# Half of a causal convolution's taps as products with diagonal tiles

## The chip, the cores and the metric

The kernel runs on one core of a Trainium2 chip. The metric is device time in microseconds (us) of one execution, as the median of several runs. TensorE (PE in the profile) multiplies tiles and writes PSUM; VectorE (DVE), ScalarE (ACT) and GpSimd (POOL) work element by element; SyncE (SP) issues the transfers.

## What is computed

A block with three mixers side by side (causal depthwise convolution, pooling, differential attention) and a routed mixture of 16 experts is followed by two layers of another kind. 256 tokens pass through it. The change touches the convolution of the first block only:

```
u = a_val * sigmoid(a_gate)                      # [256 tokens, 256 channels]
y[t, ch] = b_dw[ch] + sum over j of w[j, ch] * u[t - 30 + j, ch]     # 31 taps, zeros before t = 0
y = silu(layer_norm(y)); y @ w_pw + b_pw
```

All of it is float32. `a_val` and `a_gate` are columns of the product of the normed input with `w_in`, as are the inputs of the pooling and the attention's q, k and v. The three mixers' outputs, side by side, are multiplied by `w_out` and added to the residual.

## The kernel before

Activations lie with features on the 128 partitions and tokens along the row. Each weight is cut into two parts, a rounded one (`h`, on ScalarE, line 361) and the rest (`l`, on VectorE or for some sections on GpSimd, line 377), and each product of a 128x128 weight tile is three matmuls (lines 485 to 487). Weights stream in, in order of use, and are split six chunks of four tiles ahead of the products, into 9 buffers for `h` and 7 for `l`.

The order of the first block's work is written as a weave. A generator (`fillers`) puts out the products, and after every four weight tiles (12 matmuls) there is a tick. At a tick, work that was put off with `after(n, ...)` comes due, `conv_tick` takes one step of each running convolution, and up to two attention events are taken (scores, turned probabilities, values). What comes out is an order of emission; a scheduler of the compiler turns it into one fixed order for each engine, and may move an instruction ahead when what it needs is there.

The products of `w_in` come in this order: the values (a section of its own, ticks 2 to 9), then 14 output tiles of two ticks each: q0, k0, a0, gate 0, a1, gate 1, q1, k1, q2, k2, q3, k3, p0, p1 (ticks 10 to 37). Each output tile is summed in one of the four PSUM buffers of the pool `mm`. The norm's factor for each token (line 605: `norm_rows`) is worked out by a chain of small VectorE instructions (lines 524 to 537) at the start of the 14 tiles. The convolution of channels 0 to 127 starts when gate 0 is done (tick 17), the other half at tick 21. Heads 0 and 1 of the attention get their q and k normed after k1, heads 2 and 3 after k3, each by a chain of small VectorE instructions (`norm_qk`) and products with them (line 598).

A step of a convolution is one tap on VectorE: `y = u * w + y` over 128x256 (line 983). Of the 31 taps, 18 go this way. The other 13 are multiplied on ScalarE (lines 972 and 977) and added up on GpSimd (line 978), one in each of the first steps; a last VectorE addition (line 985) joins the two sums. Two steps after both halves are done the layer norm follows (`conv_norm`). Then come the products with `w_pw` and `w_out`, which wait for the mixers' outputs, the last of them for the last two heads of the attention.

Of the kernel before, what the change touches and what calls it, by code (L numbers as in the profile page):

```python
# [36 lines left out]
TAPS = 18  # L37
# [3 lines left out]
# ---------------------------------------------------------------- tile order  # L41
def order(ms, kc, first):
    """Output tiles `ms` over kc input chunks: the first group chunk by chunk, the rest
    one output tile after the other."""
    out = [(k, m) for k in range(kc) for m in ms[:first]]
    for m in ms[first:]:
        out += [(k, m) for k in range(kc)]
    return out
# [17 lines left out]
def moe_order():  # L66
    """Weight pieces of the experts as they are used: ("in", e), and ("down", e) LAG experts later."""
    out = []
    for e in range(16 + LAG):
        out += [("in", e)] if e < 16 else []  # L70
        out += [("down", e - LAG)] if e >= LAG else []
    return out
# [5 lines left out]
def z_columns():  # L78
    """Columns of w_in_2 for each tile of Z_MS; in branches A and C chunk i holds heads i and i + 4.
    Rotary partners lie 32 features apart."""  # L80
# [16 lines left out]
def sections():  # L97
    """The weight stream, section by section: name, number of 128x128 tiles."""
# [16 lines left out]
# ---------------------------------------------------------------- host layout  # L115
def cut(w, plan, rows=None, cols=None):
    """Tiles [n, 128, 128] of w in the order of plan."""
# [58 lines left out]
def columns(v):  # L176
    """A vector over features as columns of 128 features."""
# [40 lines left out]
def lay_rpb(rpb):  # L218
    """[layers, pairs, query chunks, 128, 2 heads, T]: bias of every key, NEG where it isn't seen."""
# [12 lines left out]
def shared_tables():  # L232
    """Constants that depend on shapes alone, up to 128 rows each."""
# [85 lines left out]
# ---------------------------------------------------------------- the program  # L319
class Stream:  # L320
    """Weights in order of use: loaded ahead, cut in two parts a few chunks ahead of the products."""
# [12 lines left out]
    def widen(self, pool, bufs, until):  # L334
        """More buffers for the units before `until`."""
# [3 lines left out]
    def load(self, to=None):  # L339
        """Units up to `to`, or as many as there is room for."""  # L340
# [29 lines left out]
    def rest(self, c):  # L370
        """The second parts of the chunks before c that have their first."""
# [18 lines left out]
class Weave:  # L390
    """Puts other work between the pieces of a run of products. An event says whether it could take place."""
# [16 lines left out]
    def run(self, fill, events=(), first=0, last=1):  # L408
        """Ticks with each piece of fill; the events are spread over ticks first to last, counted from here."""
# [18 lines left out]
class Kernel:  # L428
# [36 lines left out]
    # -------- weights  # L465
# [5 lines left out]
    def weight4(self, t):  # L471
        """Four tiles in a row, as one moving operand."""
        return self.stream.chunk(t // CHUNK)

    def mm_w(self, out, xh, xl, wh, wl, start, stop):
        """The activations stay, the weights move."""
# [12 lines left out]
    def linear(self, name, plan, kc, xh, xl, n, evac, at=0, every=0, bank=None):  # L489
        """Yields after each output tile (or every so many products); evac(m, psum) takes the sum over the kc chunks.  # L490
        n: columns, or a function of m."""
# [18 lines left out]
    # -------- small helpers  # L510
# [8 lines left out]
    def rsqrt(self, src, shape, mul, add=EPS):  # L519
        """1 / sqrt(src * mul + add)."""  # L520
# [20 lines left out]
    def head_rsqrt(self, ssq, shape):  # L541
        """From sums over a head of squares without the token's 1 / rms: the factor that norms the head,
        1 / sqrt(ssq / HD + EPS / rms ** 2)."""
        return self.rsqrt(ssq, shape, 1.0 / HD, self.eps_tok.to_broadcast(shape))

    # -------- deferred rms norm
    def norm_chunk(self, k, n, gain, square=True):
        """Chunk k of the residual: x * gain in two parts, and its square added up."""
# [26 lines left out]
    def norm_tok(self, n, bank=None):  # L575
        """1 / rms of each token, tokens on the partitions: columns of tokens 0, 128 (and T - 128) on."""
# [12 lines left out]
    def spread(self, y, n):  # L589
        """Such columns on all partitions, tokens along the row (in psum). y: [128, 3], or [128, 3, 2] for a column for each  # L590
        half of the partitions."""
# [10 lines left out]
    def norm_rows(self, n, ticks=(2, 5)):  # L602
        """1 / rms of each token on all partitions: self.rb, within the next few ticks."""
# [18 lines left out]
    # -------- block 2  # L622
    def ffn(self, f, l, n, gain, n_next, ticks=(2, 5)):
        """X += 0.5 * swiglu, then what the next norm needs (the last one has its gain applied later)."""
# [60 lines left out]
class Block1:  # L685
    """Conv, pool and differential attention mixers side by side, then the routed experts."""
# [23 lines left out]
    def small(self):  # L710
# [5 lines left out]
        # lambda and scaled gains  # L716
# [42 lines left out]
    # -------- w_in, and the three mixers between its products and those of w_out  # L759
    def mixers(self):  # L760
# [14 lines left out]
        self.after(30, self.later_tables)  # L775
        self.after(6, self.lam)
# [56 lines left out]
    def out_tiles(self, name, ks):  # L833
        """Input chunks ks of the output tiles of w_out, two of which share a bank that the first one's start clears."""
# [35 lines left out]
    def turn_tokens(self, k):  # L870
        """Chunk k of x: its part of the router's products, and tokens on the partitions in two parts."""
# [53 lines left out]
    def norm_qk(self, first):  # L925
        """Norms of q and k of two heads."""
# [13 lines left out]
    def pool_mix(self, c, z):  # L940
        """Window means over 2, 4 (chunk 0) or 8, 16 (chunk 1) tokens less the token itself."""
# [23 lines left out]

    def conv_steps(self, c):
        """The taps of chunk c one by one: the last ones are summed apart, by other engines."""
        K, nc = self.K, self.nc
        tap = lambda j: (self.u[c][:, j:j + S], K.param("conv_w", 31 * c + j))
        y, other = self.cv[c], self.one([128, S], f"cw{c}")  # L970
        u, w = tap(TAPS)
# [931 lines left out]
```

## Time and profile before

| | |
|---|---|
| time, median of 3 runs | 1694.37 us (1693.71 to 1694.73) |
| span of the profiled execution (the only time that is shown of it) | 1698.4 us |
| TensorE busy | 1629.2 us, 96% of the span |
| VectorE busy | 1235.9 us, 73% |
| ScalarE busy | 990.8 us, 58% |
| GpSimd busy | 343.9 us, 20% |

Busy times are shares of the whole span; the stretch with the convolution is about its first twelfth. Times in the rows below are counted from the start of the span. "idle before <- releaser" is how long the engine had been idle before an instruction, and what ended that.

### The profile page before, as it was taken

How to read it: one execution, taken by the hardware profiler on the slowest of the kernel's cores; microseconds unless marked ns; L12 is line 12 of the kernel's file. 1: busy time of each engine (PE TensorE's matmuls, PEld its weight loads, DVE VectorE, ACT ScalarE, POOL GpSimd, SP SyncE). 2: the span in 40 equal slices, each digit the busy share in tenths (PEclk: the TensorE clock that was granted, in tenths of full speed). 3: DMA queues.
4: the chain of work that ended last, by engine and by line, in shares of the span. 5: the costliest groups of instructions: out<-in, count | busy, mean ns of one | idle time of the engine just before them, and what ended most of it. 6: DMA issues, size and time to landing. Idle time of an engine off the chain costs nothing.

```text
span 1698.4 us, 33407 instructions
## 1 busy us (share of the span) xinstructions
PE 1629.2 (96%) x12172; PEld 1540.2 (91%) x12172; DVE 1235.9 (73%) x2625; ACT 990.8 (58%) x2050; POOL 343.9 (20%) x563
## 2 busy tenths in 40 slices
PE   8777989899999999999999999999999999999997
PEld 7767777699999988889999999999998888999997
DVE  7976999977766887656877666776688766787764
ACT  6544878755555666655655555555566666565552
POOL 2532434310000443432100000000022333210000
PEclk9877999999999999999999999999999999999999
DMA  7214888645555543444555555555554444555552
GB/s 271 100 61 162 292 278 300 227 147 174 174 174 174 169 125 115 136 154 138 180 174 174 174 174 174 174 174 174 175 163 137 131 144 142 169 184 186 184 187 82
DMA packets 87261, 289.88 MB, mean 171 GB/s; under 512 B 11696, under 2 KB 17328, under 8 KB 86960
## 3 DMA queue, kind: packets, MB, share of 16 engines
q1 hardware_dynamic: 87088, 287.66, 50.7%
q8 instruction: 98, 1.61, 0.4%
q14 instruction: 75, 0.61, 0.1%
HBM read 282.18 MB, written 1.05 MB: 167 GB/s over the span
## 4 chain that ended last, share of the span: by engine, by line
PE 58%; DVE 1%; issue 0%; DMA 0%; SPq 0%; ACT 0%; DVEq 0%; ACTq 0%
PE acc L485 18%; PE acc L487 17%; PE acc L486 17%; PE sc L1760 1%; PE po L1820 1%; PE pt L1796 1%; PE sc L1759 1%; DVE l L377 0%; PE pb L598 0%; PE pt L1806 0%; DVE xl L557 0%; PE pn L582 0%; DVE out L679 0%; DVE X L1858 0%; PE po L1817 0%
## 5 line engine op out<-in xcount | busy, mean ns | idle before, releaser
L361 ACT ACTIVATE h<-raw 128x512 fp32r<-128x512 f32 x1046 | 651.2, 631 | 536.2 <-PE acc L486 423.0
L377 DVE TENSOR_TENSOR l<-raw,h 128x512 fp32r<-128x512 f32 x981 | 718.6, 740 | 207.5 <-PE acc L487 190.9
L485 PE MATMUL acc<-xl,h 128*128 128x272 f32 (+1 forms) x2288 | 670.5, 293 | 0.1
L487 PE MATMUL acc<-xh,l 128*128 128x272 f32 (+1 forms) x2288 | 656.7, 287 | 0.0
L486 PE MATMUL acc<-xh,h 128*128 128x272 f32 (+1 forms) x2288 | 655.7, 287 | 0.0
L485 PEld LDWEIGHTS acc<-xl,h 128*128 128x128 f32 x2288 | 432.9, 189 | 14.6 <-issue 7.8
L487 PEld LDWEIGHTS acc<-xh,l 128*128 128x128 f32 x2288 | 432.3, 189 | 0.4 <-issue 0.4
L486 PEld LDWEIGHTS acc<-xh,h 128*128 128x128 f32 x2288 | 432.5, 189 | 0.2 <-issue 0.2
L573 POOL TENSOR_TENSOR sqacc<-sqacc,sq 128x272 f32<-128x272 f32 (+1 forms) x53 | 45.2, 854 | 805.5 <-ACT sq L569 804.3
L485 PE MATMUL acc<-al,h 128*128 128x272 f32 (+1 forms) x704 | 202.2, 287 | 0.0
L487 PE MATMUL acc<-ah,l 128*128 128x272 f32 (+1 forms) x704 | 202.2, 287 | 0.0
L486 PE MATMUL acc<-ah,h 128*128 128x272 f32 (+1 forms) x704 | 201.4, 286 | 0.0
L487 PEld LDWEIGHTS acc<-ah,l 128*128 128x128 f32 x704 | 132.6, 188 | 0.0
L485 PEld LDWEIGHTS acc<-al,h 128*128 128x128 f32 x704 | 132.6, 188 | 0.0
L486 PEld LDWEIGHTS acc<-ah,h 128*128 128x128 f32 x704 | 132.6, 188 | 0.0
L377 POOL TENSOR_TENSOR l<-raw,h 128x512 fp32r<-128x512 f32 x65 | 95.3, 1466 | 147.8 <-ACT h L361 39.4
L485 PE MATMUL acc<-ob,h 128*128 128x272 f32 (+1 forms) x320 | 92.7, 290 | 0.0
L486 PE MATMUL acc<-ob,h 128*128 128x272 f32 (+1 forms) x320 | 90.9, 284 | 0.0
L487 PE MATMUL acc<-ob,l 128*128 128x272 f32 (+1 forms) x320 | 90.9, 285 | 0.0
L1721 POOL TENSOR_SCALAR P<-P,r 128x272 f32<-128x272 f32 x48 | 54.9, 1144 | 160.7 <-DVE r L1719 130.6
L642 DVE TENSOR_TENSOR t<-acc,rb 128x272 f32<-128x272 f32 (+1 forms) x88 | 38.4, 436 | 63.2 <-PE acc L487 63.2
L485 PEld LDWEIGHTS acc<-ob,h 128*128 128x128 f32 x320 | 60.2, 188 | 2.3 <-issue 1.2
(381 smaller groups left out, 2212.8 us busy)
## 6 DMA issues: line engine op xcount, KB each, us to landing
raw<-in_stream_dram SPq DMA_DIRECT2D x523, 512.0 KB, 3.3
bias<-in_rpb_dram SPq DMA_DIRECT2D x16, 272.0 KB, 2.9
zs<-gates SPq DMA_DIRECT2D x48, 34.0 KB, 2.3
kk<-kk SPq DMA_DIRECT2D x24, 68.0 KB, 2.0
X<-in_x_dram SPq DMA_DIRECT2D x4, 256.0 KB, 5.8
tab<-in_tables_dram SPq DMA_DIRECT2D x1, 1024.0 KB, 7.1
zs<-gates SPq DMA_DIRECT2D x32, 32.0 KB, 2.0
out_dram<-out SPq DMA_DIRECT2D x4, 256.0 KB, 2.2
```

The costliest lines, as they stand in the source:

```text
L361: self.nc.scalar.activation(h, src, AF.Copy)
L377: engine.tensor_sub(l, src, h.bitcast(F32))
L485: mm(out, h, xl, start=start, stop=False)
L486: mm(out, h, xh, start=False, stop=False)
L487: mm(out, l, xh, start=False, stop=stop)
L573: (nc.vector if k == KC - 1 else nc.gpsimd).tensor_add(self.sqs[0], self.sqs[0], s)
L642: nc.vector.tensor_mul(u, p, rb)
L1721: (nc.gpsimd if h else nc.vector).tensor_scalar(P[:, h, keys], P[:, h, keys], r[:, h:h + 1], None, op0=ALU.mult)
L1759: nc.tensor.matmul(sc[h][:, :T], q[:, h, s], k[:, h], start=True, stop=False)
L1760: nc.tensor.matmul(sc[h][:, :T], q[p, h, s], kl[p], start=False, stop=True)
L1796: nc.tensor.transpose(p[:, 128 * (2 * c + h):128 * (2 * c + h) + 128], P[:, h, 128 * c:128 * c + 128], ident)
L1820: nc.tensor.matmul(o[64 * h:64 * h + 64], v[:, c, 64 * h:64 * h + 64], big[:, c, h, :n], start=False, stop=c == 1)
```

## The change

Sixteen of the 31 taps (the first ones) become products on TensorE: the stationary tile has the tap's 128 weights on its diagonal, the moving one is `u` shifted by the tap. The 16 products of a half are summed in one PSUM buffer of the pool `mm`, two in each of the first eight steps. The other 15 taps stay on VectorE, one in each step, with the bias in the first one, and a last VectorE addition takes the PSUM sum in. ScalarE and GpSimd have no part in the taps any more. The 32 diagonal tiles (16 KB on each partition) are made at tick 9 by GpSimd, each from the identity and a column of weights. Both operands of the new products are float32, not cut in parts.

```diff
-TAPS = 18
+TAPS = 16
...
         self.after(30, self.later_tables)
+        self.after(9, self.diagonals)
         self.after(6, self.lam)
...
+    def diagonals(self):
+        K, nc = self.K, self.nc
+        self.diag = self.one([128, 2, TAPS, 128], "diag")
+        for c in range(2):
+            for j in range(TAPS):
+                nc.gpsimd.tensor_scalar(self.diag[:, c, j], K.table("ident"), K.param("conv_w", 31 * c + j), None, op0=ALU.mult)
+
     def conv_steps(self, c):
         K, nc = self.K, self.nc
-        tap = lambda j: (self.u[c][:, j:j + S], K.param("conv_w", 31 * c + j))
-        y, other = self.cv[c], self.one([128, S], f"cw{c}")
-        u, w = tap(TAPS)
-        nc.scalar.activation(other, u, AF.Identity, scale=w, bias=K.param("conv_b", c))
-        for j in range(TAPS):
-            if j + TAPS + 1 < 31:
-                u, w = tap(j + TAPS + 1)
-                p = self.p2.tile([128, S], F32, name="tap")
-                nc.scalar.activation(p, u, AF.Identity, scale=w)
-                nc.gpsimd.tensor_add(other, other, p)
-            u, w = tap(j)
-            if j == 0:
-                nc.vector.tensor_scalar(y, u, w, None, op0=ALU.mult)
+        y = self.cv[c]
+        bank = K.mm.tile([128, T], F32, name="acc")[:, :S]
+        for i, j in enumerate(range(TAPS, 31)):
+            u, w = self.u[c][:, j:j + S], K.param("conv_w", 31 * c + j)
+            if i == 0:
+                nc.vector.tensor_scalar(y, u, w, K.param("conv_b", c), op0=ALU.mult, op1=ALU.add)
             else:
                 nc.vector.scalar_tensor_tensor(y, u, w, y, op0=ALU.mult, op1=ALU.add)
+            for t in range(2 * i, min(2 * i + 2, TAPS)):
+                nc.tensor.matmul(bank, self.diag[:, c, t], self.u[c][:, t:t + S], start=t == 0, stop=t == TAPS - 1)
             yield
-        nc.vector.tensor_add(y, y, other)
+        nc.vector.tensor_add(y, y, bank)
         yield
```

## Rows read from the trace of the kernel before

**Rows 1.** Page: busy tenths in 40 slices of 42.5 us, granted clock

```profile
PE   8777989899999999999999999999999999999997
DVE  7976999977766887656877666776688766787764
PEclk9877999999999999999999999999999999999999
```

**Rows 2.** Windows: stretch, length, busy us (instructions) by engine, granted clock, DMA

```profile
15.00:35.00 20.00, 19.12 (x140) 17.95 (x141) 14.09 (x36) 12.84 (x27) 0.63 (x1) 1.00 0.72 264
...
45.00:60.00 15.00, 12.27 (x89) 12.07 (x89) 15.00 (x22) 12.57 (x31) 14.63 (x16) 0.89 0.29 100
60.00:65.00 5.00, 0.00 (x0) 0.00 (x0) 5.00 (x15) 1.56 (x4) 1.83 (x3) 0.72 0.16 49
...
85.00:95.00 10.00, 3.40 (x26) 2.97 (x26) 9.22 (x28) 2.15 (x4) 5.33 (x6) 0.73 0.27 95
95.00:140.00 45.00, 36.44 (x220) 32.27 (x217) 31.13 (x129) 20.23 (x60) 13.76 (x13) 0.77 0.21 71
...
35.00:95.00 60.00, 43.66 (x326) 40.47 (x326) 55.17 (x131) 33.19 (x83) 33.09 (x35) 0.84 0.36 117
```

**Rows 3.** Groups by line and shape, 0 to 150 us: busy us, mean ns

```profile
L983 DVE SCALAR_TENSOR_TENSOR cv<-u,par,cv 128x256 f32<-128x256 f32 x34 | 23.8, 713 | 0.0
...
L978 POOL TENSOR_TENSOR cw<-cw,tap 128x256 f32<-128x256 f32 x24 | 21.9, 932 | 24.8 <-ACT tap L977 24.5
...
L977 ACT ACTIVATE tap<-u,par 128x256 f32<-128x256 f32 x24 | 11.9, 504 | 3.7 <-POOL cw L978 3.3
```

**Rows 4.** VectorE in order of time: start us, us, instruction

```profile
49.02 1.75 DVE L983 SCALAR_TENSOR_TENSOR cv<-u,par,cv 128x256 f32<-128x256 f32 x2
50.70 1.22 DVE L377 TENSOR_TENSOR l<-raw,h 128x512 fp32r<-128x512 f32 x1
...
64.28 0.47 DVE L983 SCALAR_TENSOR_TENSOR cv<-u,par,cv 128x256 f32<-128x256 f32 x1
...
64.76 0.68 DVE L377 TENSOR_TENSOR l<-raw,h 128x512 fp32r<-128x512 f32 x1
```

**Rows 5.** GpSimd in order of time, from 10 us

```profile
10.61 0.31 POOL L743 CAST all<-core 128x128 bf16<-128x128 f32 x1 [0.99 <-DMA core<-in_core_dram]
...
23.70 0.63 POOL L586 TENSOR_SCALAR eps<-rsa 128x2 f32<-128x2 f32 x1 [8.91 <-DVE rsa L524]
37.80 2.04 POOL L978 TENSOR_TENSOR cw<-cw,tap 128x256 f32<-128x256 f32 x2 [13.47 <-ACT tap L977]
```

**Rows 6.** Line 1721 on GpSimd: ns min/median/max, first and last start

```profile
L1721 POOL TENSOR_SCALAR P<-P,r x48: 962/1054/1775, 588.6 to 1439.7; 128x272 f32<-128x272 f32 x48
```

**Rows 7.** VectorE in order of time: a norm's chain, first and last of 12, and a later chain

```profile
23.45 0.15 DVE L524 TENSOR_SCALAR rsa<-pn 128x2 f32<-128x2 f32 x1
...
25.93 0.16 DVE L537 SCALAR_TENSOR_TENSOR rsy<-rst,rsy 128x2 f32<-128x2 f32 x1
...
102.94 1.34 DVE L533 SCALAR_TENSOR_TENSOR rst<-rsy,rsh 128x1 f32<-128x1 f32 x2
```

**Rows 8.** TensorE in order of time

```profile
20.82 0.28 PE L485 MATMUL acc<-xl,h 128*128 128x256 f32 x1
...
22.23 0.50 PE L582 MATMUL pn<-core,sqacc 128*128 128x1 f32 x4
...
26.15 0.71 PE L598 MATMUL pb<-core,rsy 128*128 128x128 f32 x4 [0.48 <-DVE rsy L537]
...
65.67 1.97 PE L598 MATMUL pb<-core,rsy 128*64 128x128 f32 x16 [6.69 <-DVE rsy L537]
...
93.29 0.58 PE L485 MATMUL acc<-pool0l,h 128*128 128x256 f32 x1 [6.60 <-DVE pool0l L963]
...
110.51 1.03 PE L1005 MATMUL pm<-cv,core 128*128 128x256 f32 x4
111.38 0.61 PE L1111 MATMUL po<-v,PT 128*128 128x128 f32 x4
```

## The prediction

> **What bounds the kernel now.** I read the page's slices first: the whole is bound by TensorE (nines nearly everywhere), but the first four slices, 170 us, are not. There TensorE stands at 7 or 8 tenths and its clock at 7 or 8, while VectorE shows 9s and a 6 [rows 1]. The change lies in these slices, so what it is worth must be read there. The views after that are windows over 15 to 140 us [rows 2], the groups of the taps [rows 3], and the engines' instructions in order of time [rows 4, 5, 7, 8].
>
> The windows show three parts. From 15 to 35 us TensorE sets the pace (19.12 of 20 us busy; VectorE 14.09, GpSimd 0.63). From 35 to 95 us VectorE does: it is busy 55.17 of 60 us, all of 45 to 65 us, and TensorE only 43.66 [rows 2]. TensorE's long waits there all end on VectorE: 6.69 us before 65.67 us, for the norm of heads 0 and 1, whose small instructions are queued among the taps, and 6.60 us before 93.29 us, for the pooling's chain [rows 8]. Idle engines have a second price: the granted clock is 0.72 in 60 to 65 us and 0.73 in 85 to 95 us, against 1.00 in 15 to 35 us [rows 2]. From 95 to 140 us no engine is full (TensorE 36.44, VectorE 31.13 of 45 us): this is the attention's last heads, one short step after another.
>
> Why VectorE is full can be seen in two pairs of rows. While GpSimd adds taps (14.63 of 15 us busy in 45 to 60 us), two taps take 1.75 us and the cut of a weight chunk 1.22 us; a few microseconds later, with GpSimd quiet, the same take 0.47 and 0.68 us [rows 2, 4]. So an instruction of VectorE waits for one of GpSimd. The mean tap takes 713 ns [rows 3].
>
> **VectorE, ScalarE and GpSimd in 35 to 95 us.** VectorE loses three taps in each half, 6 x 0.47 = 2.8 us. The 28 scalar_tensor_tensor taps that stay fall from 713 to some 470 ns: 6.8 us. The weight chunks and small instructions that now wait for GpSimd give back some 4 us (in 45 to 60 us four chunks at 0.55 us each, the rest in chains like that of 102.94 us [rows 4, 7]). In sum 13 to 14 us of 55.17, so VectorE would be some 42 of 60 us busy and no longer the bound. The last addition reads PSUM instead of SBUF at about the same price. ScalarE loses 24 multiplications of 504 ns and the two with the bias, 13 us; GpSimd loses 21.9 us [rows 3]. Neither set the pace, so these are worth only what they held up: VectorE, counted already.
>
> **TensorE in 35 to 95 us.** New are 32 products of 128x256 in float32. The nearest row is the mean of the layer norm, L1005, the same shape and type: two products are four instructions, and from its start at 110.51 us to the next line's at 111.38 us are 0.87 us, so 0.435 us for one product at a full clock [rows 8]. 32 of them: 13.9 us. For comparison a tick's 12 matmuls take 1.41 us (20.82 to 22.23 us) [rows 8], so a step of one convolution adds 0.87 us to a tick, and where both run a tick grows from 1.41 to 3.15 us.
>
> What can hide them is TensorE's idle time: 60 - 43.66 = 16.3 us [rows 2], and about 2 us that a slow clock took (16 small products in 1.97 us at 65.67 us [rows 8]; I take the same work at full clock as half to three quarters of it, and there are several). Not all of that can be filled. The norm's chain for heads 0 and 1 and the pooling's chain stay, each a dozen dependent steps; unhindered, a chain of the first kind took 2.6 us (23.45 to 26.09 us) [rows 7], of which part lies beside two ticks of products. I leave 4 to 5 us of waits (1 us and 2 us for the two chains, 1 to 2 us for the rest). So 13.9 - (16.3 + 2 - 4.5) = about 0: the stretch would take as long as before, with TensorE as its bound in place of VectorE. Bounds: -5 us if the waits vanish, +8 us if only the half of the idle time can be used.
>
> **The diagonal tiles, in 10 to 35 us.** GpSimd does not run anything from 14.8 to 37.8 us but one small instruction [rows 5], and u is ready only at about 36 us, so the 32 tiles seem free. Their price: GpSimd's own tensor_scalar of 128x272 takes 962 ns at best [rows 6], a cast of 128x128 0.31 us [rows 5]; by size I take 0.55 us, 18 us in all (10 to 23). An instruction of line 743, emitted much later, ran at 10.61 us [rows 5], so the tiles may begin there too; from 10.6 or from 20 us on, they lie over 23.45 to 26.09 us. There TensorE waits for the chain of the first norm, 0.48 us already before 26.15 us [rows 7, 8], with nothing of its own to do instead. Its 12 instructions have nine with two SBUF operands. Line 533 shows what one of them can pay when GpSimd runs: two in 1.34 us at 102.94 us instead of 0.35 [rows 7], about 1 us for one wait behind an instruction of some 1.3 us; behind one of 0.55 us I take 0.4 us. Nine waits are 3.6 us, bounds 0 (if these GpSimd instructions, with one operand, hold nothing up) and 5. I take 3 us. The cuts of weight chunks are slowed too, but they run six chunks ahead, and 8 us of lead covers that.
>
> The Trainium skill (SBUF — State Buffer, section Who interferes with whom) has a rule on just this: a VectorE instruction with two SBUF inputs contends with a GpSimd instruction that reads SBUF, and the second to come waits for the whole of the first. The rows with the additions agree (1.75 for two taps against 0.47 for one). They show GpSimd instructions with two inputs only; by the rule those with one input block as well, which would make it 3.6 us, while without it the term is 0.
>
> **From 95 us on.** The layer norm of the convolution is emitted three ticks earlier (16 steps in place of 19). It then falls beside the norms of heads 2 and 3 instead of beside the values' norms at 115 us. That shifts some 5 us of VectorE's work in a stretch that has 14 us free; I count 0, from -3 to +3 us. The transfers are no term: DMA is 0.36 busy in 35 to 95 us [rows 2], and no new transfer is issued. Behind 140 us everything waits for this stretch (the experts need the router, it needs the residual), so a shift carries to the end undiminished.
>
> **Sum.** 0 + 3 + 0 = +3 us, within the profiled execution of 1698.4 us; that is 4.0 us above the runs' median, and I take the same difference for both: 1694.4 + 2.6, rounded, 1697.0 us. A measurement of this kernel can tell about 0.2% (3.4 us), so the likeliest case straddles "no change" and "slightly slower". Its own range is 1693 to 1702 us.
>
> **Rivals.**
> 1. Faster: TensorE, fed by a VectorE that is never late, fills nearly all of its 16.3 us, keeps the full clock, and enters the last heads early; the diagonal tiles hold nothing up. For it: the waits named above are both on VectorE, and GpSimd falls silent just there. Against it: 13.9 of the 16.3 us are used up by the new products. 13.9 - 16.3 - 2 + 1 = -3.4 us, -3 us from behind 95 us, and -2 us for the chain of heads 2 and 3, which meets a lighter VectorE: -8.4, 1686 us. It decides if the terms for tiles and waits are both under 1 us.
> 2. Slower: two of four PSUM buffers. Each convolution holds one buffer of `mm` from its first step to its last addition, 16 ticks; over some twelve ticks both do, and the output tiles of q1 to q3 have two instead of four. Then a tile can only begin when the one two before it has been read out by ScalarE, which was busy 12.57 of 15 us there [rows 2]. Against it: a tile lasts 2.8 us or more, and ScalarE gets 13 us lighter. If each of six tiles waits 1.5 us, that is +9 us on +3: 1706 us; from 3 us on (0.5 us for a tile) the sign is settled.
> 3. It evens out: the tiles' cost is hidden, the stretch is as long as before: 1694.4 us.
>
> **How the numbers follow.** The forecast has 0.45 (of it 0.22 within 0.2%, 0.21 slower, 0.02 faster), rival 1 0.27 (0.26 faster, 0.01 within), rival 2 0.17 (slower), rival 3 0.11 (0.09 within, 0.02 faster). Faster 0.30, within 0.2% 0.32, slower 0.38. The range for 8 in 10 takes in most of rival 1 and the lower part of rival 2: 1685 to 1704 us.
>
> **What would show it.** Taps at 0.47 us throughout, VectorE under 45 of 60 us in 35 to 95 us; 64 new matmul instructions at about 0.22 us; no wait of 6 us before line 598 or before the pooling's product, and a granted clock near 1.00 to 95 us. For the tiles: 32 instructions of about 0.55 us on GpSimd before 37 us, and TensorE's wait at line 598 near 26 us grown from 0.48 to some 3.5 us. Wrong would be: that wait unchanged (then rival 1 or 3); TensorE idle in front of output tiles of q1 to q3 with ScalarE as the releaser (rival 2); or the stretch from 95 to 140 us, which I left as it is, longer or shorter by more than 3 us, for its many short steps follow an order that the scheduler makes anew.

## The result, and the profile after

The changed kernel takes 1712.8 us (median of 4 runs, 1705.93 to 1714.56), the kernel before 1694.55 us (1693.71 to 1695.23): a ratio of 1.010, 95% interval 1.0083 to 1.0116. It is slower by some 18 us (14 to 20). The prediction said 1697 us, range 1685 to 1704. Its profiled execution took 1713.05 us, with a span of 1711.0 us. In the page's slices of 42.8 us TensorE has fallen in the first from 8 tenths to 6 and risen in the second from 7 to 9, VectorE has fallen in both, and the clock is up from 7s to 8s [rows 1]:

```profile
PE   6977989989999999999999999999999999999997
...
DVE  5775999977766886656877666776678766787764
...
PEclk9988999999999999999999999999999999999999
```

The windows that answer to [rows 2], with the same columns:

```profile
15.00:35.00 20.00, 15.87 (x95) 13.88 (x96) 11.88 (x29) 11.35 (x25) 20.00 (x26) 0.91 0.56 211
35.00:95.00 60.00, 54.77 (x413) 50.13 (x411) 44.80 (x128) 24.18 (x61) 10.70 (x15) 1.00 0.40 126
95.00:140.00 45.00, 32.91 (x195) 28.14 (x195) 31.50 (x115) 18.79 (x54) 15.35 (x14) 0.77 0.14 49
```

From 35 to 95 us the prediction's picture is there: VectorE 44.80 us busy, under the 45 forecast, TensorE the bound with 54.77, its clock at 1.00. But the stretch begins late: from 15 to 35 us TensorE was busy 15.87 us where it had been busy 19.12, beside a GpSimd that is never idle. The groups that answer to [rows 3] (line, engine, forms, count, busy us, mean ns, idle before): 

```profile
L987 PE MATMUL acc<-u,diag 128*128 128x256 f32 x64 | 16.6, 386 | 2.9 <-DVE u L898 2.9
...
L985 DVE SCALAR_TENSOR_TENSOR cv<-u,par,cv 128x256 f32<-128x256 f32 x28 | 13.5, 483 | 0.8
```

A tap has fallen from 713 to 483 ns. Matmuls overlap, so the price of a product is read from starts: from the products of one tick to those of the next are 2.25 us (46.36 to 48.61 us in TensorE's order of time), a tick without lasts 1.41 [rows 8], so a product is 0.42 us against 0.435 forecast:

```profile
46.36 1.02 PE L987 MATMUL acc<-u,diag 128*128 128x256 f32 x4
...
48.61 1.03 PE L987 MATMUL acc<-u,diag 128*128 128x256 f32 x4
```

Where the time went is clearest from four landmarks: the end of the values' products (the first matmul of line 485, at 20.82 us in [rows 8]), the first addition of the mixers' output to the residual (146.85 us before), the norm's sums (line 582) near 1230 us and the next such sums near 1495 us. The table gives the first as a time and the others as the distance from the one before, with every kernel of the experiments below. What follows the last landmark is 198 us in each. One execution of e10_twelve took 5486.88 us and one of e12_wrapped 2250.31 us; the ratios leave these two out, and without them the medians would be 1695.64 and 1697.09 us.

| kernel | median us | values end | to residual | to 1230 | to 1495 |
|---|---|---|---|---|---|
| before | 1694.55 | 20.82 | 126.03 | 1088.01 | 265.54 |
| before_again | one run, 1694.93 | 20.59 | 124.40 | 1084.41 | 265.33 |
| after | 1712.8 | 25.62 | 130.72 | 1087.97 | 268.89 |
| e4_tiles_alone | 1699.08 | 25.72 | 126.34 | 1084.37 | 265.31 |
| e1_tiles_later | 1702.15 | 21.32 | 130.21 | 1087.12 | 267.61 |
| e2_two_products | 1696.75 | 27.70 | 119.51 | 1087.57 | 264.73 |
| e8_step_later | 1709.38 | 25.59 | 126.07 | 1084.93 | 267.71 |
| e3_norm_later | 1703.86 | 25.70 | 127.89 | 1084.22 | 268.87 |
| e5_three | 1694.84 | 20.87 | 120.97 | 1084.39 | 267.47 |
| e7_all_vector | 1691.5 | 20.71 | 121.13 | 1084.46 | 265.36 |
| e9_four | 1687.45 | 20.84 | 116.01 | 1085.41 | 265.21 |
| e6_eight | 1686.85 | 20.71 | 114.94 | 1088.62 | 265.20 |
| e10_twelve | 1695.92 | 20.99 | 118.02 | 1089.29 | 268.17 |
| e11_pushed | 1689.0 | 21.29 | 114.45 | 1084.54 | 267.50 |
| e12_wrapped | 1697.14 | 25.05 | 120.93 | 1084.33 | 265.80 |

Against the profile of before: +4.8 us by the values' end, +4.7 to the residual, 0 to 1230 us, +3.4 to 1495 us, 12.6 us in all after the tail's -0.2. The other 5.5 us up to the medians' 18 are in the kernel before, as a second profile of it shows:

> The kernel before, unchanged, for a second profile of it: every theory expects the landmarks of the first one within 1 us up to 150 us (values' products done at 20.8 us, the first block's last sum at 146.9 us), and a span within 5 us of 1698.4 us.

It took 1694.93 us, close to the median, with a span of 1692.9: 5.5 us less than the execution that the prediction was worked out on, 1.9 by the residual and 3.6 before 1230 us, more than expected of two executions of one kernel. Against this profile the changed kernel's is 18.1 us longer: 5.0, 6.3, 3.6, 3.6 and a tail of -0.4. The 3.6 us on the way from the residual to 1230 us are as much as two executions of the kernel before differ there, so they can't be put down to the change; the last section returns to them.

**The first 5 us: tiles between the sums of squares.** GpSimd of the changed kernel, in order of time, from the place of [rows 5] (two earlier additions lie before these rows):

```profile
10.38 1.81 POOL L973 TENSOR_SCALAR diag<-core,par 128x128 f32<-128x128 f32 x2 [0.67 <-DMA core<-in_core_dram]
12.16 0.74 POOL L573 TENSOR_TENSOR sqacc<-sqacc,sq 128x256 f32<-128x256 f32 x1
12.88 3.09 POOL L973 TENSOR_SCALAR diag<-core,par 128x128 f32<-128x128 f32 x5
15.95 0.71 POOL L573 TENSOR_TENSOR sqacc<-sqacc,sq 128x256 f32<-128x256 f32 x1
16.64 3.28 POOL L973 TENSOR_SCALAR diag<-core,par 128x128 f32<-128x128 f32 x4
19.89 0.72 POOL L573 TENSOR_TENSOR sqacc<-sqacc,sq 128x256 f32<-128x256 f32 x1
20.59 0.60 POOL L973 TENSOR_SCALAR diag<-core,par 128x128 f32<-128x128 f32 x1
21.16 0.73 POOL L573 TENSOR_TENSOR sqacc<-sqacc,sq 128x256 f32<-128x256 f32 x1
21.87 16.32 POOL L973 TENSOR_SCALAR diag<-core,par 128x128 f32<-128x128 f32 x20
```

GpSimd runs its instructions in the order that the scheduler fixed, and twelve tiles stand among the additions that sum the squares for the first norm (line 573). ScalarE, which makes those squares, waits:

```profile
12.93 0.42 ACT L569 ACTIVATE sq<-X 128x256 f32<-128x256 f32 x1 [1.18 <-POOL sqacc L573]
16.69 0.42 ACT L569 ACTIVATE sq<-X 128x256 f32<-128x256 f32 x1 [3.34 <-POOL sqacc L573]
17.01 1.13 ACT L361 ACTIVATE h<-raw 128x512 fp32r<-128x512 f32 x2
20.65 0.42 ACT L569 ACTIVATE sq<-X 128x256 f32<-128x256 f32 x1 [2.50 <-POOL sqacc L573]
20.97 2.18 ACT L361 ACTIVATE h<-raw 128x512 fp32r<-128x512 f32 x4
```

Three waits, 7.0 us; behind the second and the third stand cuts of weights (line 361) in ScalarE's order, and for the first of those cuts TensorE waits 3.33 us, first in the rows that answer to [rows 8]:

```profile
17.68 0.79 PE L478 MATMUL acc<-h,xl 128*128 128x512 f32 x1 [3.33 <-ACT h L361]
...
25.62 0.28 PE L485 MATMUL acc<-xl,h 128*128 128x256 f32 x1
...
31.51 0.71 PE L598 MATMUL pb<-core,rsy 128*128 128x128 f32 x4 [1.05 <-DVE rsy L537]
...
41.73 1.10 PE L987 MATMUL acc<-u,diag 128*128 128x256 f32 x4 [1.54 <-DVE u L898]
...
54.11 1.10 PE L987 MATMUL acc<-u,diag 128*128 128x256 f32 x4 [1.35 <-DVE u L898]
...
96.34 1.97 PE L598 MATMUL pb<-core,rsy 128*64 128x128 f32 x16 [3.69 <-DVE rsy L537]
...
108.32 0.44 PE L1105 MATMUL pt<-core,P 128*128 128x128 f32 x2 [2.26 <-ACT t L1122]
...
109.86 0.41 PE L485 MATMUL acc<-mix,h 128*128 128x256 f32 x1
...
129.04 0.66 PE L1134 MATMUL pt<-core,osb 128*128 128x128 f32 x2 [4.92 <-DVE osb L1127]
```

Behind the wait of 3.33 us the granted clock is 0.81 up to 25.62 us, where the values' products had run at 1.00 before; the first six products behind it start 0.43 us apart instead of 0.23, which takes 1.2 us more.

The wait that the prediction put at line 598 (26.15 us before, 31.51 now) grew from 0.48 to 1.05 us, not to 3.5. VectorE's chain ahead of it, first and last:

```profile
28.60 0.15 DVE L524 TENSOR_SCALAR rsa<-pn 128x2 f32<-128x2 f32 x1
...
31.29 0.16 DVE L537 SCALAR_TENSOR_TENSOR rsy<-rst,rsy 128x2 f32<-128x2 f32 x1
```

The other waits of these rows are the next part: for `u`, ahead of the first products of the two halves, 2.9 us in all (41.73 and 54.11), 3.69 us for the norm of the heads, 2.26 us behind it, and 4.92 us in the last heads. The row at 109.86 us is the first product with the mixers' outputs; in the kernel before it is

```profile
101.13 0.28 PE L485 MATMUL acc<-mix,h 128*128 128x256 f32 x1
```

### The profile page after: what moved, and what is told of

The parts are those of the page before. It is cut to its first block, busy times and chain, and to the rows that moved or that the text cites. A ratio compares the mean times of both kernels' runs of the same rounds, so it can differ in the third digit from the quotient of the medians.

```text
span 1711.0 us, 33517 instructions
## 1 busy us (share of the span) xinstructions
PE 1642.1 (96%) x12236; PEld 1550.2 (91%) x12236; DVE 1228.6 (72%) x2619; ACT 979.9 (57%) x2024; POOL 344.2 (20%) x571
## 3 DMA queue, kind: packets, MB, share of 16 engines
HBM read 282.18 MB, written 1.05 MB: 166 GB/s over the span
## 4 chain that ended last, share of the span: by engine, by line
PE 58%; DVE 1%; DMA 0%; issue 0%; ACT 0%; SPq 0%; DVEq 0%; ACTq 0%
PE acc L485 18%; PE acc L487 17%; PE acc L486 17%; PE sc L1764 1%; PE po L1824 1%; PE pt L1800 1%; PE sc L1763 1%; PE pb L598 0%; PE pt L1810 0%; DMA zs<-gates 0%; PE pn L582 0%; DVE out L679 0%; PE po L1821 0%; DMA kk<-kk 0%; PE ph L1620 0%
## 5 line engine op out<-in xcount | busy, mean ns | idle before, releaser
L485 PEld LDWEIGHTS acc<-xl,h 128*128 128x128 f32 x2288 | 433.6, 190 | 14.5 <-issue 7.9
```

Source lines behind the costliest of these rows:

```text
L485: mm(out, h, xl, start=start, stop=False)
```

## The experiments

**The tiles alone.** The kernel before, with the 32 tiles made at tick 9 and read by nothing:

```diff
+        self.after(9, self.diagonals)
...
+        for c in range(2):
+            for j in range(16):
+                nc.gpsimd.tensor_scalar(self.diag[:, c, j], K.table("ident"), K.param("conv_w", 31 * c + j), None, op0=ALU.mult)
```

> The kernel before, with the 32 diagonal tiles made as in the changed kernel, and used by nothing. Theory A: the values' products end at about 25.6 us in place of 20.8, and the whole takes 4 to 6 us more than before, about 1699 us. Theory B or C alone: no more than 1 us, 1695 us.

1699.08 us, ratio 1.0026 (1.0013 to 1.0040). ScalarE waits the same 1.18, 3.34 and 2.50 us, the values end at 25.72 us, and all else is as in the second profile of before but for 1.9 us on the way to the residual. The tiles cost 5 us without any product.

**The tiles later.** The changed kernel, with the tiles made to need the first norm's sum, so that they can't stand among the additions:

```diff
-        self.after(9, self.diagonals)
+        self.after(11, self.diagonals)
...
+        zero, cw = self.one([128, 1], "zero"), self.one([128, 62], "cw")
+        nc.gpsimd.tensor_scalar(zero, K.radicand[:, 0:1], 0.0, None, op0=ALU.mult)
+        nc.gpsimd.tensor_scalar(cw, K.param("conv_w", 0, 62), zero, None, op0=ALU.add)
...
-                nc.gpsimd.tensor_scalar(self.diag[:, c, j], K.table("ident"), K.param("conv_w", 31 * c + j), None, op0=ALU.mult)
+                nc.gpsimd.tensor_scalar(self.diag[:, c, j], K.table("ident"), cw[:, 31 * c + j:31 * c + j + 1], None, op0=ALU.mult)
```

> The changed kernel, with the diagonal tiles made only after the first norm's sum is read (their weights pass through two small GpSimd instructions that depend on it), so that none of them stands between the additions of the squares. Theory A (in the changed kernel the tiles stand between these additions on GpSimd, so ScalarE waits to hand over the next square, the weight cuts behind it come late, and the products of the values end 4.8 us late, at 25.6 us in place of 20.8): the values' products end at about 20.8 us again, and the whole takes 4 to 5 us less than the changed kernel, about 1708 us. Theory B (the lost time comes from the new products on TensorE alone): no change, 1713 us. Theory C (it comes from the layer norm's earlier place): no change, 1713 us.

1702.15 us, ratio 1.0046 (1.0029 to 1.0063). The values end at 21.32 us, 4.3 us earlier, and the residual comes 4.8 us earlier. The median fell by 10.7 us, twice what was expected; the runs of the changed kernel lie up to 8.6 us apart, and I can't assign the rest. GpSimd now makes the tiles without a pause beside the taps:

```profile
26.33 23.52 POOL L976 TENSOR_SCALAR diag<-core,cw 128x128 f32<-128x128 f32 x32
```

A tile takes 0.74 us, not 0.55. So the taps of one half meet GpSimd and those of the other don't. VectorE's group of taps in 37 to 50 us of this kernel, and then in 50 to 64 us:

```profile
L988 DVE SCALAR_TENSOR_TENSOR cv<-u,par,cv 128x256 f32<-128x256 f32 x14 | 7.7, 550 | 0.4
```

```profile
L988 DVE SCALAR_TENSOR_TENSOR cv<-u,par,cv 128x256 f32<-128x256 f32 x14 | 6.8, 484 | 0.4
```

550 ns against 484: beside GpSimd's instruction with one input a tap takes a seventh longer. Beside its additions with two inputs two taps took 1.75 us [rows 4].

**Without the products.** The changed kernel with only the products of taps 0 and 15 of each half; the other 28 are left out and computed nowhere, so this is a measure of time alone:

```diff
-            for t in range(2 * i, min(2 * i + 2, TAPS)):
+            for t in {0: [0], 7: [TAPS - 1]}.get(i, []):
```

> The changed kernel with 2 instead of 16 products for each half (taps 0 and 15; the other 14 taps of TensorE's are left out). All tiles are still made. 28 products of 0.435 us go, 12.2 us of TensorE's work. Theory B (TensorE sets the pace from 42 to 92 us and the new products lie on the path): the 14 output tiles end about 12 us earlier than at 92.4 us, and the whole takes 8 to 12 us less, about 1703 us. Theory A or C alone (the products fill idle time): under 3 us less, about 1711 us.

1696.75 us, ratio 1.0019 (1.0008 to 1.0031). From the values' end to the residual it is 119.51 us, 11.2 less than with all products; 28 x 0.42 = 11.8 us were left out. So next to nothing of them was hidden: on TensorE, 54.77 of 60 us busy, the last products cost nearly their full price. (The values end 2.1 us later in this execution, in which ScalarE waited 1.26 us for the first weights, so the distance is the fair measure; by the clock the residual comes 9.1 us earlier.) The two waits for `u` stayed (1.54 and 1.28 us). The median fell by 16.1 us where 8 to 12 were expected: another 4.2 us come off behind 1230 us (264.73 instead of 268.89), which is the subject of the last experiments.

**Products one step later.** The first products of a half are emitted with the step in which `u` is still being made, and stand in TensorE's order ahead of a tile that could run:

```diff
-            for t in range(2 * i, min(2 * i + 2, TAPS)):
+            for t in range(max(2 * i - 2, 0), min(2 * i, TAPS)):
```

> The changed kernel with one edit: each pair of products comes one step later than the tap beside it, so that the first pair of a half no longer stands in TensorE's order ahead of a tile's matmuls while u is not yet there. Tiles and layer norm stay as in the changed kernel (values' products end near 25.6 us). If TensorE's two waits for u (1.54 and 1.35 us) are a cost of their own, they vanish, the 14 output tiles end some 2.9 us earlier than in the changed kernel, and the time falls from 1712.8 to some 1709.5 to 1711. Rival: the products only move, and TensorE, short of work elsewhere, waits as long at another place: the 14 tiles end within 1 us of the changed kernel's and the time stays within 1711.5 to 1714.

1709.38 us, ratio 1.0094 (1.0075 to 1.0114). TensorE in order of time, where 41.73 and 54.11 us were:

```profile
41.93 1.10 PE L987 MATMUL acc<-u,diag 128*128 128x256 f32 x4
...
54.07 1.89 PE L987 MATMUL acc<-u,diag 128*128 128x256 f32 x8
```

Both waits are gone, and the residual comes 4.7 us earlier. Of these, 2.9 us, as much as the two waits, are gained by the time when ScalarE reads out k3, the twelfth of the 14 tiles (the pooling's two follow). Its read-out in the kernel before, in the changed one and in this one:

```profile
78.85 0.37 ACT L907 ACTIVATE zk<-acc 128x256 f32<-128x256 f32 x1
```

```profile
88.43 0.36 ACT L908 ACTIVATE zk<-acc 128x256 f32<-128x256 f32 x1
```

```profile
85.56 0.38 ACT L908 ACTIVATE zk<-acc 128x256 f32<-128x256 f32 x1
```

The waits were a cost of their own. The medians alone would not show it: they are 3.4 us apart, and the two intervals of the ratio overlap. What gave the other 1.8 us behind k3 was not traced to one cause.

**The layer norm later.** With 16 steps in place of 19 the convolution's layer norm is emitted three ticks earlier. Undone:

```diff
-        self.after(1, mean)
-        self.after(2, var)
+        self.after(4, mean)
+        self.after(5, var)
```

> The changed kernel with the convolution's layer norm put off by three ticks, so that it is emitted at the tick of the kernel before. Theory C (its earlier place puts VectorE work and waits among the last heads of the attention, where 95 to 140 us lost another 4 us): 3 to 5 us less, about 1709 us. Theories A and B: no change, 1713 us.

1703.86 us, ratio 1.0056 (1.0039 to 1.0073). The way to the residual is 2.8 us shorter, net of waits that grew elsewhere. TensorE's wait of 4.92 us in the last heads has become

```profile
125.34 0.30 PE L1134 MATMUL pt<-core,osb 128*128 128x128 f32 x1 [1.64 <-DVE osb L1127]
```

Of the median's fall of 9 us that leaves 6: the profile is 3.8 us shorter before 1230 us too, but two profiles of one kernel differ there almost as much, so I can't assign them.

**All three.** Tiles later, products one step later, layer norm later, each as above:

> The changed kernel with three edits together: the tiles made after the first norm's sum, the layer norm three ticks later, and each pair of products put out one step later, so that TensorE does not come to them before u is there (1.5 us of waiting in each half). If theories A and C are right and their times add, the first block's last sum is done about 4.8 + 2.8 us earlier than in the changed kernel, and another 2 to 3 us for u: 146 to 147 us in place of 156.3, as in the kernel before (146.9), and the whole takes about 1694 to 1697 us. If the edits only uncover each other's waits (theory B: TensorE is full anyway), 1700 us or more.

1694.84 us, ratio 1.0003 (0.9992 to 1.0014): no change against the kernel before. To the residual it is 120.97 us, 3.4 and 5.1 less than in the two profiles of before, and it is reached at 141.84 us, 5 us earlier than expected. The change freed of its three costs does shorten its stretch; 2.1 us of that are lost again behind 1230 us.

**How many taps.** GpSimd can be freed of the taps without TensorE: all 31 taps on VectorE, two in each of the first twelve of 19 steps, no tiles. And with the tiles late and one product in each step from the second one, TensorE can take 4, 8 or 12 taps of 31, VectorE the others in 18 steps (two in each of the first ones, so that with the last addition there are 19 steps and the layer norm falls at the tick of the kernel before, three later than in the changed kernel). First the edit to the kernel before for all on VectorE, then that to the changed kernel:

```diff
-        for j in range(TAPS):
-            if j + TAPS + 1 < 31:
...
-                nc.gpsimd.tensor_add(other, other, p)
...
+        for i in range(19):
+            for _ in range(2 if i < 12 else 1):
+                u, w = self.u[c][:, j:j + S], K.param("conv_w", 31 * c + j)
...
-        nc.vector.tensor_add(y, y, other)
```

```diff
-TAPS = 16
+TAPS = 8    # or 4, or 12
...
-        for i, j in enumerate(range(TAPS, 31)):
+        j, steps = TAPS, 18
+        for i in range(steps):
+            for _ in range(2 if i < 31 - TAPS - steps else 1):
...
-            for t in range(2 * i, min(2 * i + 2, TAPS)):
+            if 0 < i <= TAPS:
+                t = i - 1
```

> The kernel before with all 31 taps on VectorE, in 19 steps (two in each of the first 12), nothing on ScalarE, GpSimd or TensorE. If VectorE was filled by waiting for GpSimd, 62 x 0.47 = 29 us against 24.3 us plus 4 us of slower weight cuts, and the whole takes as long as before, within 3 us, about 1694 us. If the waiting for GpSimd cost little, VectorE gets 13 x 2 x 0.47 = 12 us more on the path: about 1706 us.

> Eight taps on TensorE and 23 on VectorE in 18 steps (two in each of the first five), tiles made after the first norm's sum, one product in each step from the second on, layer norm at the tick of the kernel before. TensorE gets 7 us of products in place of 13.9, VectorE 16 taps more than the changed kernel, 46 x 0.47 = 21.6 us, still less than the 24.3 us that 34 taps took beside GpSimd's additions. Theory B: the balance moves back from TensorE, and the whole takes 4 to 8 us less than the kernel before, about 1688 us. If VectorE's taps, not GpSimd's additions, were what filled it, the stretch gets no shorter than before: 1694 us or more.

> As the kernel with eight taps on TensorE, but four on TensorE and 27 on VectorE (two in each of the first nine steps). Theory: with GpSimd silent, TensorE and VectorE share the stretch and the best split is where both are nearly full; VectorE, 55.7 of 60 us busy at eight, gets eight taps of 0.48 us more (59.6 of 60), so it is the bound again: 1688 to 1691 us, towards the 1691.5 us of all 31 on VectorE. Rival: every product taken from TensorE helps, since it is the bound of the whole program: 8 x 0.435 = 3.5 us less, some 1683.5 us.

> As the kernel with eight taps on TensorE, but twelve on TensorE and 19 on VectorE (two in the first step, then one). Theory of the two bounds: TensorE, 52.9 of 60 us busy at eight, gets 8 x 0.435 = 3.5 us more (56.4 of 60, as with sixteen and the three edits) while VectorE has some 4 us to spare: 1689 to 1692 us, between the 1686.85 us of eight and the 1694.84 us of sixteen with three edits. Rival: only GpSimd's silence counts and the split does not: within 2 us of 1686.85 us, as four would be too.

| taps on TensorE | 0 | 4 | 8 | 12 | 16 (all three edits) |
|---|---|---|---|---|---|
| median us | 1691.5 | 1687.45 | 1686.85 | 1695.92 | 1694.84 |
| ratio to before | 0.9981 (0.9970 to 0.9993) | 0.9961 (0.9949 to 0.9972) | 0.9955 (0.9941 to 0.9970) | 1.0007 (0.9997 to 1.0017) | 1.0003 (0.9992 to 1.0014) |
| TensorE, VectorE busy in 35 to 95 us | 45.58, 57.13 | 50.46, 54.18 | 52.89, 55.73 | 53.11, 49.95 | 56.43, 46.83 |
| values' end to residual | 121.13 | 116.01 | 114.94 | 118.02 | 120.97 |

All on VectorE is 3.1 us faster than before: handing 13 of the 31 taps to ScalarE and GpSimd had bought no time. From 20 to 150 us VectorE is busy 101.76 us with all of them, where it had been 100.25 with 18. Why the time even fell was not separated: ScalarE lost its multiplications and the taps come two to a step as well. The window from 35 to 95 us of that kernel and of the one with eight:

```profile
35.00:95.00 60.00, 45.58 (x353) 40.44 (x352) 57.13 (x168) 24.19 (x63) 13.39 (x13) 0.85 0.35 117
```

```profile
35.00:95.00 60.00, 52.89 (x411) 47.30 (x409) 55.73 (x171) 26.09 (x71) 17.72 (x18) 0.94 0.37 122
```

With eight both engines are nearly full, and the way to the residual is 6 us shorter than at either end of the table. Eight beats both kernels, by 7.8 and 26 us. Four, which I expected 1 to 4 us slower, is level with it (their intervals overlap); twelve is 4 us slower than expected, and its own stretch, 3.1 us longer than with eight, explains a third of the 9 us between them; another third is next.

**The last 3 us, far behind.** In the last column of the table the kernels fall into two groups: 264.7 to 265.8 us, and 267.5 to 268.9 us for those with 24 or 32 products (counting e11 below). In the second group VectorE waits some 1.2 to 1.5 us for transfers of line 1525 (`zs<-gates`; the line differs by kernel), and in the first group not at all; TensorE later waits 2.1 to 2.4 us for `kk`, in the first group 0 to 1.6. What differs ahead of it is where a transfer of 0.02 MB on the instruction queue falls: 12.5 to 13 us behind the norm's sums near 1230 us in that group, 14.5 to 18 us in the other (before e12 below), the earlier the more products. To test it, the kernel with eight got 16 small products that nothing reads, at the very start, where TensorE is idle at first (it runs them until 7.92 us, where its first product had begun at 7.10):

```diff
+        idle, bank = self.one([128, 129], "idle"), K.mm.tile([128, 512], F32, name="acc")
+        nc.vector.memset(idle, 0.0)
+        for _ in range(16):
+            nc.tensor.matmul(bank[:, :1], idle[:, :128], idle[:, 128:], start=True, stop=True)
```

> The kernel with eight taps on TensorE, and 16 products of 128x1 with zeros put at the very start of TensorE's program, before its first matmul at 7.10 us, where it is idle; nothing reads them. In all thirteen profiles so far a transfer of 0.02 MB on the instruction queue falls 12.5 to 18 us behind the norm near 1230 us, the earlier the more products the kernel has, and in the six kernels where it falls at 12.5 to 13 us (24 or 32 products) VectorE then waits 1.2 to 1.5 us for the line of the transfers zs from gates, and the next norm near 1490 us comes 267.5 to 268.9 us behind the last one, against 264.7 to 265.5 us in the seven others. Theory: the place of that transfer does it, set by the number of TensorE instructions ahead. With 16 products more (32 in all, as in the changed kernel) it moves from 14.5 to some 12.5 us, VectorE waits 1.2 to 1.5 us for zs, and the distance goes from 265.2 to some 268 us: 1686.85 + 2.5, 1688.5 to 1690.5 us. Rival: the convolution's own order or its tiles do it: distance 265.2 us, time within 1 us of 1686.85.

1689.0 us, ratio 0.9974 (0.9962 to 0.9987), 2.2 us above the kernel with eight by the medians, whose intervals just overlap; the clear sign is the distance, 267.50 instead of 265.20 us. VectorE at the first `zs` in the kernel with eight, and here:

```profile
1238.54 1.01 DVE L1542 TENSOR_TENSOR zs<-zs,tab 128x272 f32<-128x272 f32 x1
```

```profile
1235.82 0.44 DVE L1546 TENSOR_TENSOR zs<-zs,tab 128x272 f32<-128x272 f32 x1 [1.17 <-DMA zs<-gates]
```

The queues (packets, MB, share of 16 engines) in the half microsecond with the instruction transfer, 14.5 us behind the sums with eight and 12.5 us here:

```profile
q8 instruction: 1, 0.02, 11.5%
q1 hardware_dynamic: 29, 0.01, 10.7%
```

```profile
q1 hardware_dynamic: 93, 0.08, 53.2%
q8 instruction: 1, 0.02, 11.5%
```

With eight the other queue has nearly run dry; here the transfer falls into the middle of its work. The opposite test: the kernel with all three edits and 24 such products (`range(24)` in the same place), to carry the transfer ahead of `zs`.

> The changed kernel with all three edits (tiles later, products one step later, layer norm later), and 24 products of 128x1 with zeros at the very start of TensorE's program, where it is idle; nothing reads them. It has 32 products, the transfer on the instruction queue at 12.5 us behind the norm and a distance of 267.5 us to the next. Theory: with 56 products in all the transfer falls some 6 us earlier, ahead of the transfers zs from gates, which begin 10 us behind the norm: no wait for zs, distance 265 to 265.5 us, and the time falls from 1694.84 by some 2.3 us to 1692 to 1693.5. Rival: as above, distance 267.5 us and 1694 to 1696 us.

The transfer fell 6 us behind the sums, VectorE did not wait for `zs`, and the distance went from 267.47 to 265.80 us. The median rose all the same, to 1697.14 us, ratio 1.0025 (1.0011 to 1.0038): the small products held TensorE until 11.34 us, so that the kernel's first one began 4.3 us late (values' end 25.05 instead of 20.87, 4.2 us). 1694.84 + 4.2 - 1.7 = 1697.3 us.

## Why the prediction was wrong

Its sum was 0 + 3 + 0, for the stretch from 35 to 95 us, the tiles, and the stretch behind. Measured were some 5 us by the values' end, 5 from there to the residual, and 3 behind 1230 us, which the sum didn't have, against the profile that it was worked out on; and 5.5 us more because that execution was not the typical one. (Its last line also adds 2.6 where the terms give 3.)

- **The tiles, +3: 5 us, by another way.** The step that failed is "GpSimd does not run anything from 14.8 to 37.8 us ... so the 32 tiles seem free", with the cost sought in the first norm's chain on VectorE. I saw that the tiles may begin at 10.6 us and did not ask what GpSimd still had to do between 10.6 and 14.8: the sums of squares, on which ScalarE, the weights and TensorE depend. Nor did the "8 us of lead" of the weight cuts cover it: at 14.35 us TensorE had no cut weights left. e4 and e1 show it from both sides. That the size, 5 us, lies near the forecast of 3 is luck. The chain itself took 2.85 us (28.60 to 31.45 us) against 2.64 [rows 7], 0.2 us more and not the 3.6 of nine waits. The rule of the Trainium skill (SBUF — State Buffer, section Who interferes with whom) that the second instruction waits for the whole of the first agrees with the additions, but not with these tiles: 0.55 against 0.48 us for a tap with two inputs.
- **35 to 95 us, 0: the work was right, the waits left were not.** Products 0.42 us (0.435 forecast), taps 483 ns, clock 1.00: each as forecast; VectorE 44.80 us, under the 45 of the sign, though the sum said some 42. "I leave 4 to 5 us of waits" failed. The window itself shows 5.2 us of TensorE idle, but it begins 5 us late in the work. Over the same work, from the values' end to the first product with the mixers' outputs, it is 84.2 us (25.62 to 109.86) against 80.3 (20.82 to 101.13), and TensorE's waits in it, behind that for the first norm, fell from 16.4 us to 9.3 (1.54, 1.35, 3.69, 2.26 and 0.46), not to 4.5. I gave the chains 3 us; the one before 96.34 us alone took 3.69, and the 2.9 us for `u` were not among them. I had checked what products add to a tick, and not what the first of them waits for, nor what stands behind them in TensorE's order. e8 gives 4.7 us back. The upper bound of +8 does not come out of its own words either: 13.9 less half of the 16.3 us of idle time is 5.8.
- **From 95 us on, 0: outwardly right.** From k3's read-out to the residual it is 67.9 us, as before (68.0), and from the first product with the mixers' outputs 46.5 us (45.7). The total hides a cost: e3 shows that the earlier layer norm took 2.8 us, within the bound of 3. That it came out near 0 is luck; what gave as much back I did not look into.
- **Behind 140 us "a shift carries to the end undiminished": not so.** 3.4 us were added behind 1230 us. e11 adds 2.3 us there by instructions that nothing reads, and e12 takes 1.7 away by more of them; the rest of the 3.4 is open.
- **"I take the same difference for both."** That failed too: by the other profiles an execution's time is 2 us more than its span (1713.05 and 1711.0, 1694.93 and 1692.9), so the execution of 1698.4 us was some 6 us above its median, and the changed kernel's is within 0.3 us of its own.

Rival 2, two of four PSUM buffers, did not happen: no wait of TensorE for ScalarE's read-out stands in 35 to 95 us. Rival 1's mechanism, a TensorE that VectorE hardly keeps waiting, came nearest with eight taps, half of the products: up to the last of the 14 tiles its waits are 0.42 us, but behind them one stands as long as in the kernel before (6.69):

```profile
85.50 1.76 PE L598 MATMUL pb<-core,rsy 128*64 128x128 f32 x14 [6.58 <-DVE rsy L537]
```

With all 16 and the three costs taken away the way to the residual is 3.4 to 5.1 us shorter than before, some 2 of them are lost behind 1230 us, and the time is that of before: the products used up most of the 16.3 us of idle time, as the argument against rival 1 said.

## What to carry to other kernels

That an engine is idle on average does not make work on it free: look at each chain that passes through it, and give the work a dependency that keeps it out of the chain. Likewise an instruction put into a full engine's order needs its inputs at the moment when that engine reaches it, or all behind it wait. When load is moved from a full engine to another, look for the split at which both are nearly full; here a quarter of the taps was enough, and 3.1 of the 7.8 us gained came without any product, with the taps taken off GpSimd and ScalarE.

## What the runs showed of the hardware

Adding instructions to TensorE's program moved a transfer on the instruction queue 1.2 ms later, and where it fell among the transfers of `zs` it cost 2.3 us; the profile shows it as waits of VectorE and TensorE for transfers that the change doesn't touch. That the collision of the two transfers is what delays `zs` is inferred from their place; that the number of TensorE's instructions ahead moves it is shown by e11 and e12.

The way from the residual to 1230 us takes 1084.2 to 1085.4 us in some profiles and 1087.1 to 1089.3 in others, whatever the kernel. In the two profiles of the kernel before, the window that begins 100 us behind the first addition to the residual reads:

```profile
246.85:256.85 10.00, 10.00 (x43) 8.37 (x44) 7.59 (x12) 6.15 (x11) 2.59 (x2) 0.85 0.73 251
```

```profile
244.99:254.99 10.00, 10.00 (x49) 8.31 (x49) 8.53 (x14) 7.63 (x13) 3.33 (x3) 1.00 0.79 277
```

The granted clock was 1.00 (2.4 GHz) in the second, and 0.85 in the first, which has some of the window at 1.2 GHz: 43 matmuls against 49, with TensorE busy throughout in both. In the ten microseconds ahead it had been busy 7.87 and 7.95 us, so what it did there doesn't tell the two apart; 70 us later the clock was 0.76 and 0.96. A difference of 3.6 us between two single profiles says nothing of two kernels.
